# Two transformer blocks on one core: the FFN up-projection meets both halves of its activations in one matmul, the compression runs on unsplit fp32, the keys are padded with zeros

## The chip, the core and the metric

The kernel runs on one core of a Trainium2 chip. A core has a matrix engine (TensorE, PE in the profile; its weight loads stand apart as PEld), a vector engine (VectorE, DVE), a scalar engine (ScalarE, ACT), GpSimd (POOL) and an engine that here only issues DMAs (SyncE, SP). They run side by side and wait for one another through semaphores. The metric is the device time of one execution in microseconds, median of three runs.

## The reference, cut to what matters

256 tokens of width 1024 go through two layers of a first block and two of a second. Everything is fp32. What the change touches:

```python
def compress(t, pe, w1, b1, w2, b2):          # keys and values, per kv group
    ...                                       # 15 blocks of 32 tokens, stride 16
    flat = blocks.transpose(0, 1, 3, 2, 4).reshape(B, nc, G, CMP_LEN * D)   # 2048 wide
    h = jax.nn.gelu(flat @ w1 + b1)           # 2048 -> 256
    return h @ w2 + b2

s_s = einsum('bqgrd,bgqkd->bgrqk', qb, k_g) * scale    # selected keys; 8 heads, 2 key groups of 64
s_w = einsum('bqgrd,bkgd->bgrqk', qb, kwb) * scale     # window keys

def conv_ffn(x, w_up, conv_w, conv_b, w_down):         # first block, D_FF = 2816
    h = x @ w_up                                       # 1024 -> 2 * 2816
    hc = conv_b
    for k in range(CONV_WIDTH):                        # 3 taps along the tokens
        hc = hc + hp[:, k:k + S] * conv_w[k]
    g, up = jnp.split(hc, 2, axis=-1)
    return (jax.nn.silu(g) * up) @ w_down

gu = h @ w_ffn_gu                                      # second block, the same widths, no taps
ffn = (jax.nn.silu(gu[..., :D_FF_2]) * gu[..., D_FF_2:]) @ w_ffn_down
```

## The kernel before

Large products are made in a shortened fp32 (`F32R`). Each fp32 operand is split into a high half and a low half, and a product is the sum of three: high by high, high by low, low by high. `split` makes the halves of a weight tile `raw` of 128x1024 (`wh` by a cast, `wl` by a subtraction), `put_split` those of an activation; these stand in tiles `x` of class `X4`, high and low in a tile each. Small products (attention scores, masks, the second product of the compression) take fp32 as it is, and the profile shows each such matmul as two PE instructions.

`ffn` goes over 22 feature tiles of 128 (`ft`), two to a step. For gate and up (`gu`) it loads 128 columns of `w_up`, splits them, and `up_mm` makes 8 x 3 matmuls of 256 columns (the 256 tokens move, the weight stands still) into one half of a PSUM bank of class `upp`. One DVE instruction takes both halves out of the bank and multiplies them by the rows' norm factor `R`. In the first block come the three taps (`conv`), then silu, the product, the split into `ah` and `al`, and `down_mm`: 12 matmuls of 512 columns per `ft` into four banks, `pa` for the first 128 tokens (`t` = 0) and `pb` for the second. The last four `ft` are held back, and all their `t` = 0 matmuls are asked for before those of `t` = 1, so that the norm of the first tokens can begin early; two of these four have their weights in `x` tiles (`spare`). In the second block the first four `ft` are made another way (`linear`), so 36 of 44 products go through `up_mm` there.

`first_mix` is the attention part of the first block. `compress_g` runs twice a layer: it gathers 30 columns per 128 of the 2048 inputs, splits them, splits four tiles of weights, and makes 16 x 2 matmuls (60 and 30 stationary columns, 256 moving) into one bank; `pair_sum` adds the two halves afterwards. `qk_g` transposes the keys into `kT`, whose rows 0 to 63 are group 0 and rows 64 to 127 group 1, and `attend_g` multiplies 64 rows of `qT` by 64 rows of `kT`.

The order is not the program's. A recorder collects all operations, and `schedule` places them with costs of its own: each engine takes the ready operation of least priority number, which is its place in the program plus an entry of the table `SHIFT`; `HOLD` delays one, and `ALT` names operations that go to another engine (a cast from ACT to DVE, a product from DVE to POOL). Tiles come from classes with a fixed number of slots. Every operation is emitted from one line, so all rows of the profile say L522, and one goes by tile names.

Of the kernel before, what the change touches and what calls it, by code (L numbers as in the profile page):

```python
# [516 lines left out]
def emit(nc, order):  # L517
    for op in order:
# [9 lines left out]
        (0, 0): 11, (0, 2): -701  # L528
    },
# [5 lines left out]
    },  # L535
# [5 lines left out]
    },  # L541
    "f1m": {
        (1, 0): -520, (1, 1): -3630, (1, 2): -723, (2, 0): -251, (2, 1): 188, (2, 2): -699
    },
# [11 lines left out]
    },  # L556
# [5 lines left out]
    },  # L562
    "f2m": {
        (1, 0): -676, (1, 1): -278, (1, 2): -631, (2, 1): -3, (2, 2): -666
    },
# [23 lines left out]
    },  # L589
# [47 lines left out]
    },  # L637
    "s": {
        (0, 0): 76, (0, 2): 156
    },  # L640
    "s2": {
        (0, 0): 185
# [57 lines left out]
        386, (13, 0): 1023, (13, 2): 251, (15, 0): 2398, (15, 1): 1400, (18, 2): 643  # L700
    },
}
ALT = {
    "f1": {
        79, 137, 148, 149, 216, 217
    },
# [1305 lines left out]
```

## Time and profile before

| | |
|---|---|
| median of three runs | 1586.02 us (1585.66 to 1587.5) |
| span of the profiled execution | 1583.9 us |
| of the span, PE busy | 99% |
| DVE, ACT, POOL busy | 68%, 48%, 31% |
| granted PE clock | 1.00 in every stretch but the last (0.97) |
| read from HBM | 267.94 MB |

The runs' median lies 2.1 us above the span, and that is taken to stay. The stages follow one another: mixing of layer 1 to about 153 us, its FFN to 342, its gate, then the same for layer 2 to about 700, then twice mixing (260 us) and FFN of the second block. A busy time on PE counts matmuls that overlap, so the mean of one matmul (283 ns for 256 columns) is not what it costs; that is the distance from its start to the next one's start.

### The profile page before, as it was taken

The numbers are of one execution on the slowest core, as the hardware profiler recorded it, in microseconds if no ns is written. First come the engines' busy times: TensorE is split into PE (matmuls) and PEld (weight loads), VectorE is DVE, ScalarE is ACT, GpSimd is POOL, SyncE is SP. The second block draws the span as 40 slices with busy tenths as digits, with TensorE's granted clock in tenths as the row PEclk, the third lists the DMA queues.
The fourth block names the chain that finished last, engine by engine and source line by source line (L and its number), as shares of the span: only waits on it lengthen the run. The fifth ranks groups of instructions, "written<-read, shape, count | busy, mean of one in ns | idle before, by whom it ended". The sixth has DMA issues, their size and how long they took to land.

```text
span 1583.9 us, 24617 instructions
## 1 busy us (share of the span) xinstructions
PE 1562.3 (99%) x9421; PEld 1358.9 (86%) x9421; DVE 1083.7 (68%) x1582; ACT 761.7 (48%) x1333; POOL 492.3 (31%) x428
## 2 busy tenths in 40 slices
PE   7999999999999999999999999999999999999998
PEld 6778999988778999988888888999988888889997
DVE  6777877888777877886645647566566455675664
ACT  4566555554666545556453444323354534343242
POOL 2433111122433111115233552323443326424233
PEclk9999999999999999999999999999999999999999
DMA  8643765745644656736534556566555344555571
GB/s 271 221 147 103 216 186 176 217 129 172 202 128 129 211 180 189 211 121 194 180 109 132 166 186 193 172 188 188 163 183 186 107 139 160 193 173 174 178 224 38
DMA packets 264091, 270.60 MB, mean 171 GB/s; under 512 B 11698, under 2 KB 196645, under 8 KB 263973
## 3 DMA queue, kind: packets, MB, share of 16 engines
q1 hardware_dynamic: 263972, 269.03, 55.0%
q8 instruction: 74, 1.21, 0.3%
q14 instruction: 45, 0.36, 0.1%
HBM read 267.94 MB, written 1.05 MB: 170 GB/s over the span
## 4 chain that ended last, share of the span: by engine, by line
PE 96%; DVE 2%; ACT 1%; DMA 1%; SPq 0%; issue 0%; POOL 0%; DVEq 0%; POOLq 0%; ACTq 0%
PE pa L522 36%; PE upp L522 35%; PE pb L522 19%; PE trp L522 5%; DMA raw<-in_w_in_dram 1%; DVE wl L522 1%; DVE u L522 1%; SPq L522 0%; ACT L522 0%; ACT u L522 0%; ACT junk L522 0%; DVE x L522 0%; DVE wh L522 0%; ACT x L522 0%; POOL sm L522 0%
## 5 line engine op out<-in xcount | busy, mean ns | idle before, releaser
L522 ACT CAST wh<-raw 128x1024 fp32r<-128x1024 f32 (+3 forms) x382 | 393.0, 1033 | 470.3 <-PE upp L522 234.1
L522 DVE TENSOR_TENSOR wl<-raw,wh 128x1024 fp32r<-128x1024 f32 (+3 forms) x402 | 500.5, 1257 | 119.2 <-ACT wh L522 114.5
L522 PE MATMUL upp<-x,wh 128*128 128x256 f32 x2560 | 479.3, 283 | 0.0
L522 PE MATMUL pa<-wh,x 128*128 128x512 f32 (+1 forms) x1280 | 425.9, 402 | 3.7 <-DVE x L522 2.0
L522 PEld LDWEIGHTS upp<-x,wh 128*128 128x128 f32 x2560 | 406.3, 191 | 6.2 <-ACT wh L522 0.3
L522 PE MATMUL upp<-x,wl 128*128 128x256 f32 x1280 | 361.3, 283 | 1.5 <-DVE wl L522 1.5
L522 POOL TENSOR_TENSOR wl<-raw,wh 128x1024 fp32r<-128x1024 f32 (+2 forms) x94 | 228.7, 2436 | 282.8 <-ACT wh L522 121.7
L522 PEld LDWEIGHTS pa<-wh,x 128*128 128x128 f32 x1280 | 236.7, 189 | 53.2 <-ACT u L522 2.6
L522 PE MATMUL pa<-wl,x 128*128 128x512 f32 (+1 forms) x640 | 251.9, 401 | 0.0
L522 PEld LDWEIGHTS upp<-x,wl 128*128 128x128 f32 x1280 | 244.6, 191 | 3.4 <-DVE wl L522 2.0
L522 POOL TENSOR_TENSOR u<-u,u 128x256 f32<-128x256 f32 (+4 forms) x98 | 109.3, 1117 | 328.0 <-ACT u L522 288.0
L522 DVE CAST wh<-raw 128x1024 fp32r<-128x1024 f32 (+3 forms) x114 | 89.3, 787 | 100.3 <-PE pa L522 38.7
L522 PE MATMUL pb<-wh,x 128*128 128x512 f32 (+2 forms) x496 | 157.4, 384 | 0.0
L522 PEld LDWEIGHTS pa<-wl,x 128*128 128x128 f32 x640 | 120.8, 189 | 21.4 <-DVE u L522 0.8
L522 DVE TENSOR_TENSOR u<-upp,u 128x512 f32<-128x512 f32 x80 | 55.2, 690 | 72.4 <-PE upp L522 71.6
L522 PEld LDWEIGHTS pb<-wh,x 128*128 128x128 f32 x496 | 90.4, 188 | 15.8 <-ACT wh L522 0.6
L522 PE MATMUL pb<-wl,x 128*128 128x512 f32 (+2 forms) x248 | 92.2, 381 | 0.0
L522 PE MATMUL trp<-c_ident,u 128*128 128x128 f32 (+4 forms) x415 | 79.5, 274 | 2.6 <-DMA u<-in_pre_mix_g_dram 1.9
L522 POOL TENSOR_TENSOR sm<-sm,c_nhalf 128x1 f32<-128x1 f32 (+1 forms) x60 | 47.9, 799 | 106.3 <-DVE sm L522 104.3
L522 DVE SCALAR_TENSOR_TENSOR u<-u,c_cols_conv_w,u 128x254 f32<-128x254 f32 (+1 forms) x176 | 73.5, 478 | 0.0
L522 ACT ACTIVATE u<-u 128x256 f32<-128x256 f32 (+1 forms) x100 | 44.5, 445 | 55.5 <-DVE u L522 49.6
L522 POOL TENSOR_TENSOR al<-u,ah 128x256 fp32r<-128x256 f32 x22 | 22.6, 1027 | 148.0 <-ACT ah L522 78.0
(209 smaller groups left out, 2092.3 us busy)
## 6 DMA issues: line engine op xcount, KB each, us to landing
raw<-in_w_in_dram SPq DMA_DIRECT2D x112, 512.0 KB, 4.0
raw<-in_w_up_dram SPq DMA_DIRECT2D x88, 512.0 KB, 4.2
raw<-in_w_ffn_gu_dram SPq DMA_DIRECT2D x88, 512.0 KB, 4.8
raw<-in_w_down_dram SPq DMA_DIRECT2D x44, 512.0 KB, 4.4
raw<-in_w_ffn_down_dram SPq DMA_DIRECT2D x44, 512.0 KB, 4.1
raw<-in_w_o_dram SPq DMA_DIRECT2D x32, 512.0 KB, 4.0
raw<-in_cmp_w_dram SPq DMA_DIRECT2D x16, 512.0 KB, 4.9
raw<-in_w_ple_gate_dram SPq DMA_DIRECT2D x16, 512.0 KB, 3.9
```

The lines of the kernel that those rows point to most:

```text
L522: f(*args, **kw)
```

## The change

- `up_mm`: high and low activations now lie side by side in one tile of class `X8` (four of 2048 in place of nine `X4` of 1024). The high weight meets both in one matmul of 512 columns, the low weight the high half in one of 256. Gate goes to a bank of `upp`, up to one of `trp`; a copy (ACT) and an addition (DVE) join the two halves of each bank, and the multiplication by `R` then reads SBUF.
- `compress_g`: no split. The 30 columns are padded to 32, and 16 fp32 matmuls of 32 stationary columns write four groups of 32 PSUM partitions; `pair_sum` adds the four and now has 128 rows.
- `kT` becomes two tiles, one for each key group, with zeros in the other group's 64 rows; the scores use all 128 rows.
- new tables `SHIFT`, `HOLD`, `ALT`.

```diff
 SHIFT = {
     "c1": {
-        (0, 0): 11, (0, 2): -701
+        (0, 0): 333, (0, 2): -3277
...
-    c["pair_sum"] = np.concatenate([np.eye(30, dtype=f), np.eye(30, dtype=f)], axis=0)
+    c["pair_sum"] = np.concatenate([np.eye(32, 30, dtype=f)] * 4, axis=0)
...
-    X4 = cls("x4", 9, 1024, F32R, reserve=2)
+    X8 = cls("x8", 4, 2048, F32R, reserve=1)
...
     def xtile():
-        xh = X4.tile([128, 4, 256])
-        xl = X4.tile([128, 4, 256])
-        return xh, xl
+        both = X8.tile([128, 4, 2, 256])
+        return both[:, :, 0], both[:, :, 1], both
...
-                nc.tensor.matmul(ps, hv[:, k], xh, start=(k == 0), stop=False)
-                nc.tensor.matmul(ps, hv[:, k], xl, start=False, stop=False)
-                nc.tensor.matmul(ps, lv[:, k], xh, start=False, stop=(k == 7))
+                xx = xs[k // 4][2][:, k % 4]
+                nc.tensor.matmul(ps, hv[:, k], xx.rearrange("p a n -> p (a n)"), start=(k == 0), stop=(k == 7),
+                                 skip_group_check=True)
+                nc.tensor.matmul(ps[:, 0:256], lv[:, k], xx[:, 0], start=False, stop=(k == 7), skip_group_check=True)
...
-                        up_mm(ps[:, gu], hv, lv)
+                        up_mm(ps, hv, lv)
+                        nc.scalar.copy(z[:, gu], ps[:, 256:512])
+                        nc.vector.tensor_tensor(z[:, gu], ps[:, 0:256], z[:, gu], op=ALU.add)
                     if ft == nq:
                         R = spread(rs)
-                    z = unit("z").rearrange("p (a n) -> p a n", a=2)
-                    nc.vector.tensor_tensor(z, ps, bcast(R.unsqueeze(1), [128, 2, 256]), op=ALU.mult)
+                    nc.vector.tensor_tensor(z, z, bcast(R.unsqueeze(1), [128, 2, 256]), op=ALU.mult)
...
-                nc.vector.tensor_copy(kT[:, :, tok(t)], ps[:, 0:2])
+                for g in range(2):
+                    gp, go = slice(g * 64, (g + 1) * 64), slice((1 - g) * 64, (2 - g) * 64)
+                    nc.gpsimd.memset(kT[g][go, :, tok(t)], 0.0)
+                    nc.vector.tensor_copy(kT[g][gp, :, tok(t)], ps[gp, 0:2])
...
-                    hv, lv = split(load(w1[:, m0:m0 + 4]))
-                    for mm in range(4):
-                        m = 8 * mq + 4 * mh + mm
...
-                        nc.tensor.matmul(ps1[:60, :256], xs_[:, m].rearrange("p a n -> p (a n)"), hv[:, mm],
-                                         start=(m == 0), stop=(m == 15))
...
+                raw = load(w1[:, 4 * mq:4 * mq + 4])
+                for r in range(4):
+                    nc.tensor.matmul(ps1[32 * r:32 * r + 32, :256], X[:, 4 * mq + r], raw[:, r], start=(mq == 0),
+                                     stop=(mq == 3))
...
-                    nc.tensor.matmul(S[:, e], qT[t][gp, j0 + e], kT[gp, :, 0:(t + 1) * 128], start=True, stop=False)
+                    nc.tensor.matmul(S[:, e], qT[t][:, j0 + e], kT[g][:, :, 0:(t + 1) * 128], start=True, stop=False)
```

Three places show how the rows move on PE. A row says what is written, then what moves and what stands, and the moving columns. First the up-projection in the FFN of layer 1, before: three matmuls of 256 columns to each of eight pieces of `x`.

```order
L522 MATMUL upp_227<-x_80,wh_65 128x256
L522 MATMUL upp_227<-x_78,wh_65 128x256
L522 MATMUL upp_227<-x_80,wl_70 128x256
L522 MATMUL upp_228<-x_77,wh_68 128x256
L522 MATMUL upp_228<-x_81,wh_68 128x256
L522 MATMUL upp_228<-x_77,wl_74 128x256
```

The three of a piece read two `x` tiles, high and low. The same place of layer 2 in the changed kernel:

```order
L522 MATMUL trp_225<-x_77,wh_68 128x512
L522 MATMUL trp_225<-x_77,wl_73 128x256
L522 MATMUL upp_223<-x_75,wh_65 128x512
L522 MATMUL upp_223<-x_75,wl_70 128x256
...
L522 MATMUL pa_218<-wh_67,ah_107 128x512
L522 MATMUL pa_218<-wl_72,ah_107 128x512
```

Two matmuls remain of three, with the same 768 moving columns, and up-products now take banks of `trp`. Next the compression of layer 1 among the projections, before:

```order
L522 MATMUL pb_226<-wh_66,x_78 128x512
L522 MATMUL trp_230<-wh_67,x_79 60x256
L522 MATMUL trp_230<-wl_72,x_79 30x256 x2
L522 MATMUL trp_230<-wh_67,x_79 60x256
L522 MATMUL trp_230<-wl_72,x_79 30x256
```

Matmuls of 60 and 30 stationary columns alternate in one bank. In the changed kernel:

```order
L522 MATMUL trp_224<-raw_58,u_81 32x256
L522 MATMUL upp_222<-wh_68,x_75 128x280
L522 MATMUL upp_222<-wl_73,x_75 128x280
L522 MATMUL upp_222<-wh_68,x_75 128x280 x2
L522 MATMUL trp_224<-raw_58,u_81 32x256
L522 MATMUL trp_224<-raw_60,u_81 32x256 x4
L522 MATMUL upp_222<-wl_73,x_75 128x280
```

Of the 16 matmuls of this call five stand alone, and the others in runs of five and six; the two calls for the values have one run of nine, one of two and five alone. Last the end of the FFN of layer 1, where the last `ft` (here `wh_69`, `al_117`) meets the first tokens in `pa`, before:

```order
L522 MATMUL pa_223<-wl_71,ah_112 128x512
L522 MATMUL pa_223<-wh_69,al_117 128x512
L522 MATMUL pb_225<-x_75,ah_115 128x512
L522 MATMUL pb_226<-x_75,ah_115 128x512
...
L522 MATMUL pb_225<-wl_71,ah_112 128x512
L522 MATMUL trp_229<-c_ident_190,c_h_191 128x128 x4
```

After `pa` is complete 13 matmuls into `pb` stand ahead of the next norm's transposes (`trp`) and three behind their beginning, 16 in all. In the changed kernel:

```order
L522 MATMUL pa_218<-wl_74,ah_108 128x512
L522 MATMUL pa_218<-wh_69,al_113 128x512
L522 MATMUL pb_220<-wh_69,ah_108 128x512
L522 MATMUL pb_221<-wh_69,ah_108 128x512
L522 MATMUL pb_220<-wl_74,ah_108 128x512
L522 MATMUL pb_221<-wl_74,ah_108 128x512
L522 MATMUL pb_220<-wh_69,al_113 128x512
L522 MATMUL pb_221<-wh_69,al_113 128x512
L522 MATMUL trp_225<-c_ident_185,c_h_186 128x128 x4
```

Six are left: ten of the 16 moved ahead of the last `ft`'s share of `pa`. The end of layer 2's FFN reads the same.

## Rows read from the trace of the kernel before

**Rows 1.** The page: span, busy time of each engine, shares of the chain that ended last.

```profile
span 1583.9 us, 24617 instructions
PE 1562.3 (99%) x9421; PEld 1358.9 (86%) x9421; DVE 1083.7 (68%) x1582; ACT 761.7 (48%) x1333; POOL 492.3 (31%) x428
PE 96%; DVE 2%; ACT 1%; DMA 1%; SPq 0%; issue 0%; POOL 0%; DVEq 0%; POOLq 0%; ACTq 0%
```

**Rows 2.** Stretches: us, busy by engine, granted clock, DMA share, GB/s; FFN of layer 1.

```profile
193.00:313.00 120.00, 120.00 (x846) 112.64 (x845) 94.86 (x138) 61.68 (x93) 15.18 (x13) 1.00 0.64 193
```

**Rows 3.** The chain in order of time: start us, us, engine and tile, matmuls.

```profile
738.35 10.00 PE pa L522 x44
...
1120.55 17.27 PE upp L522 x144
```

**Rows 4.** PE groups by form: rows*columns standing, moving form, count, busy us, mean ns, idle.

```profile
L522 PE MATMUL upp<-x,wh 128*128 128x256 f32 x2560 | 479.3, 283 | 0.0
L522 PE MATMUL upp<-x,wl 128*128 128x256 f32 x1280 | 361.3, 283 | 1.5 <-DVE wl L522 1.5
L522 PE MATMUL upp<-u,u 64*128 64x512 f32 x32 | 17.9, 640 | 0.0
L522 PE MATMUL upp<-u,u 64*128 64x256 f32 x32 | 11.1, 428 | 0.0
```

**Rows 5.** PE in order of time: start us, us, what; scores, fp32 products, `pair_sum`.

```profile
61.27 0.70 PE L522 MATMUL upp<-u,u 64*128 64x256 f32 x2
61.90 0.28 PE L522 MATMUL upp<-c_causal_b,c_ident_b 128*128 128x256 bf16 x1
...
80.21 1.12 PE L522 MATMUL upp<-u,u 64*128 64x512 f32 x2
81.26 1.10 PE L522 MATMUL pb<-u,u 128*128 128x64 f32 x8
...
86.12 0.61 PE L522 MATMUL pa<-wh,x 128*128 128x512 f32 x2
86.67 0.40 PE L522 MATMUL trp<-c_pair_sum,u 60*128 60x30 f32 x2
87.00 0.43 PE L522 MATMUL pb<-u,u 128*128 128x64 f32 x2
...
110.92 1.02 PE L522 MATMUL pa<-u,u 128*128 128x512 f32 x2
111.78 0.27 PE L522 MATMUL trp<-c_ident,u 128*128 128x128 f32 x1
...
830.43 0.59 PE L522 MATMUL upp<-u,c_gla_a 128*128 128x256 f32 x2
830.86 0.38 PE L522 MATMUL trp<-c_ident,u 128*128 128x128 f32 x2
```

**Rows 6.** PE in order of time, compression of layer 1.

```profile
35.69 0.40 PE L522 MATMUL pb<-wh,x 128*128 128x512 f32 x1
35.92 0.28 PE L522 MATMUL trp<-wh,x 128*60 128x256 f32 x1
36.04 0.40 PE L522 MATMUL trp<-wl,x 128*30 128x256 f32 x2
36.28 0.28 PE L522 MATMUL trp<-wh,x 128*60 128x256 f32 x1
```

**Rows 7.** DVE and ACT groups by form: count, busy us, mean ns, idle and its releaser.

```profile
L522 DVE TENSOR_TENSOR u<-upp,u 128x512 f32<-128x512 f32 x80 | 55.2, 690 | 72.4 <-PE upp L522 71.6
...
L522 DVE TENSOR_TENSOR u<-u,upp 128x256 f32<-128x256 f32 x8 | 3.3, 418 | 1.6 <-ACT u L522 1.6
...
L522 ACT COPY u<-trp 128x256 f32<-128x256 f32 x4 | 1.5, 369 | 1.6 <-PE trp L522 1.6
```

**Rows 8.** PE in order of time, end of the FFN of layer 1.

```profile
337.07 0.39 PE L522 MATMUL pa<-wh,al 128*128 128x512 f32 x1
...
342.73 0.47 PE L522 MATMUL pa<-wh,x 128*128 128x512 f32 x1 [0.75 <-DVE x L522]
```

More of the change, by code (lines that the diff above doesn't have):

```diff
@@ L527 @@
     "c1": {
-        (0, 0): 11, (0, 2): -701
+        (0, 0): 333, (0, 2): -3277
     },
     "f1": {
[4 rows of a table removed]
[4 rows of a table added]
     },
     "f1e": {
[4 rows of a table removed]
[4 rows of a table added]
     },
     "f1m": {
-        (1, 0): -520, (1, 1): -3630, (1, 2): -723, (2, 0): -251, (2, 1): 188, (2, 2): -699
+        (1, 0): -2776, (1, 1): -12192, (1, 2): -723, (2, 0): -132, (2, 1): 65, (2, 2): -699
     },
     "f2": {
[10 rows of a table removed]
[10 rows of a table added]
     },
     "f2e": {
[4 rows of a table removed]
[4 rows of a table added]
     },
     "f2m": {
-        (1, 0): -676, (1, 1): -278, (1, 2): -631, (2, 1): -3, (2, 2): -666
+        (1, 0): 3800, (1, 1): -303, (1, 2): 1273, (2, 0): 56, (2, 1): 5016, (2, 2): 505
     },
     "m1": {
[22 rows of a table removed]
[20 rows of a table added]
     },
     "m2": {
[39 rows of a table removed]
[37 rows of a table added]
     },
     "p1": {
[5 rows of a table removed]
[5 rows of a table added]
     },
     "s": {
-        (0, 0): 76, (0, 2): 156
+        (0, 0): 122, (0, 2): 230
     },
     "s2": {
-        (0, 0): 185
+        (0, 0): 3778, (0, 2): 419
     },
@@ L646 @@
     "c1": {
-        (0, 0): 974, (0, 2): 1486
+        (0, 0): 240, (0, 2): 1072
     },
     "f1": {
-        (3, 1): 62, (5, 0): 106, (5, 2): 7, (6, 2): 1094, (9, 2): 18, (12, 2): 519, (14, 1): 1238
+        (2, 2): 281, (3, 0): 135, (4, 2): 40, (5, 1): 366, (5, 2): 7, (6, 0): 3301, (6, 2): 155, (9, 2): 84,
+        (14, 1): 14
     },
     "f1e": {
-        (1, 0): 569, (1, 1): 203, (2, 1): 693, (3, 0): 782, (6, 0): 548, (10, 2): 7, (11, 2): 115, (12, 2): 256,
-        (14, 2): 270
+        (1, 0): 153, (2, 0): 1771, (2, 1): 13, (3, 1): 1007, (5, 1): 568, (6, 2): 49, (9, 2): 178, (11, 2): 250
     },
     "f1m": {
-        (1, 0): 1474, (1, 1): 252, (2, 1): 275
+        (1, 0): 95, (1, 1): 302, (2, 1): 664
     },
     "f2": {
[4 rows of a table removed]
[4 rows of a table added]
     },
     "f2e": {
-        (1, 1): 953, (2, 1): 1454, (3, 1): 191, (4, 1): 75, (5, 1): 294
+        (1, 1): 1210, (2, 1): 1691, (6, 0): 6, (8, 2): 293, (9, 2): 53, (10, 2): 174, (11, 2): 566, (14, 2): 49
     },
     "f2m": {
-        (1, 0): 3995, (1, 1): 715, (2, 1): 268
+        (1, 0): 1, (2, 0): 1479, (2, 1): 1079
     },
     "m1": {
[8 rows of a table removed]
[7 rows of a table added]
     },
     "m2": {
[15 rows of a table removed]
[14 rows of a table added]
     },
     "p1": {
-        (3, 2): 15, (6, 2): 4, (8, 0): 580, (8, 1): 2246, (10, 0): 1337, (10, 1): 3584, (11, 2): 70, (12, 1):
-        386, (13, 0): 1023, (13, 2): 251, (15, 0): 2398, (15, 1): 1400, (18, 2): 643
+        (3, 2): 452, (7, 1): 2054, (8, 1): 1387, (9, 0): 2083, (9, 1): 981, (10, 1): 2524, (12, 1): 1580, (13,
+        0): 2016, (13, 1): 200, (13, 2): 266, (15, 1): 2721, (18, 2): 502, (20, 2): 167
+    },
+    "s2": {
+        (0, 0): 1073
     },
@@ L703 @@
 ALT = {
+    "c1": {
+        10, 13
+    },
     "f1": {
-        79, 137, 148, 149, 216, 217
+        8, 11, 12, 61, 79, 82, 121, 127, 138, 164, 182, 194, 196
     },
     "f1e": {
-        28, 62, 224, 302, 303, 306, 336, 371, 372, 439, 504
+        1, 50, 51, 119, 120, 155, 176, 188, 244, 256, 311, 335, 367, 432
     },
     "f1m": {
-        62, 81, 142
+        110, 118
     },
     "f2": {
-        17, 31, 32, 39, 53, 145, 167, 168, 170, 226, 228, 230, 238, 279, 307, 308, 311, 349, 350, 405, 424, 482,
-        483, 520, 575, 576, 580, 621, 622, 649, 654, 674, 747, 765, 792, 793, 821, 822, 824, 896, 940, 968, 969,
-        972, 973
[3 rows of a table added]
     },
     "f2e": {
-        56, 57, 76, 103, 132, 206, 278, 280, 286, 312, 340, 342, 374, 402, 403, 407
+        19, 23, 44, 46, 106, 108, 143, 147, 168, 169, 170, 208, 209, 226, 231, 232, 237, 255, 259, 278, 280,
+        281, 309, 326, 331, 334
     },
     "f2m": {
-        1, 28, 57, 58, 76, 130, 131, 134
+        1, 22, 44, 45, 48, 49, 63, 64, 81, 102, 107, 110
     },
     "m1": {
[4 rows of a table removed]
[4 rows of a table added]
     },
     "m2": {
[6 rows of a table removed]
[7 rows of a table added]
     },
     "p1": {
-        5, 16, 32, 35, 37
+        12, 16, 31, 32, 37, 69
     },
     "s": {
-        5, 6, 9, 11
+        5, 11, 12
     },
     "s2": {
-        7, 18, 19, 21, 27, 34, 35, 36, 43
+        18, 19, 21, 32, 33, 34, 35
     },
@@ L966, in split @@
         a, n = v.shape[1], v.shape[2]
-        wh = (X4 if spare else WH).tile([128, 1024])
-        wl = (X4 if spare else WL).tile([128, 1024])
+        if spare:
+            both = X8.tile([128, 2, 1024])
+            wh, wl = both[:, 0], both[:, 1]
+        else:
+            wh, wl = WH.tile([128, 1024]), WL.tile([128, 1024])
         hv = wh[:, :a * n].rearrange("p (a n) -> p a n", a=a)
@@ L991, in mms @@
                 k = k0 + a
-                xh, xl = xs[k // 4]
+                xh, xl = xs[k // 4][:2]
                 lh, ll = xh[:, k % 4, tok(t)], xl[:, k % 4, tok(t)]
@@ L1040, in feat @@
             nc.tensor.transpose(ps[:, a], s, ident)
-        xh, xl = xt
+        xh, xl = xt[:2]
         if gains is None:
@@ L1211, in ffn @@
                 rec.group += 1
-                ps = bank(upp, "upps").rearrange("p (a n) -> p a n", a=2)
                 act = unit("act")[:, :256]
@@ L1215, in ffn @@
                 if ft >= nq:
+                    z = unit("z").rearrange("p (a n) -> p a n", a=2)
                     for gu in range(2):
                         c0 = gu * DFF + ft * 128
+                        ps = bank(trp if gu else upp, "upps")
                         hv, lv = split(load(wu[:, :, c0:c0 + 128]))
-                        up_mm(ps[:, gu], hv, lv)
+                        up_mm(ps, hv, lv)
+                        nc.scalar.copy(z[:, gu], ps[:, 256:512])
+                        nc.vector.tensor_tensor(z[:, gu], ps[:, 0:256], z[:, gu], op=ALU.add)
                     if ft == nq:
                         R = spread(rs)
-                    z = unit("z").rearrange("p (a n) -> p a n", a=2)
-                    nc.vector.tensor_tensor(z, ps, bcast(R.unsqueeze(1), [128, 2, 256]), op=ALU.mult)
+                    nc.vector.tensor_tensor(z, z, bcast(R.unsqueeze(1), [128, 2, 256]), op=ALU.mult)
                 else:
+                    ps = bank(upp, "upps").rearrange("p (a n) -> p a n", a=2)
                     for gu in range(2):
@@ L1295, in first_mix @@
         linear(xs, 8, w, 512, 1024, put_kv, pool=pa)
-        qT, kT = [], unit("kT").rearrange("p (b n) -> p b n", b=2)
+        qT, kT = [], [unit("kT").rearrange("p (b n) -> p b n", b=2) for g in range(2)]
         gates = []
@@ L1333, in compress_g @@
                     nc.tensor.transpose(ps[:, g, tok(t)], zC[t][:, a * 128:(a + 1) * 128], ident)
-            X = unit("X")
-            Xv = X[:, :480].rearrange("p (m g n) -> p m g n", m=16, g=2)
+            X = unit("X").rearrange("p (m c) -> p m c", m=16)
+            nc.gpsimd.memset(X[:, :, 30:32], 0.0)
+            Xv = X[:, :, 0:30].rearrange("p m (g n) -> p m g n", g=2)
             pe = col("cmp_pe", i, kv * 16, 16)
@@ L1345, in compress_g @@
             yield
-            xs_ = X4.tile([128, 16, 2, 30])
-            Xm = X[:, :480].rearrange("p (m n) -> p m n", m=16)
-            nc.scalar.copy(xs_[:, :, 0], Xm)
-            nc.vector.tensor_tensor(xs_[:, :, 1], Xm, xs_[:, :, 0].bitcast(F32), op=ALU.subtract)
             yield
@@ L1352, in compress_g @@
             ps1 = bank(trp, "cps")
-            for mq in range(2):
-                for mh in range(2):
-                    m0 = 8 * mq + 4 * mh
-                    hv, lv = split(load(w1[:, m0:m0 + 4]))
-                    for mm in range(4):
-                        m = 8 * mq + 4 * mh + mm
-                        if m > 0:
-                            nc.tensor.matmul(ps1[:30, :256], xs_[:, m, 0], lv[:, mm], start=False, stop=False)
-                        nc.tensor.matmul(ps1[:60, :256], xs_[:, m].rearrange("p a n -> p (a n)"), hv[:, mm],
-                                         start=(m == 0), stop=(m == 15))
-                        if m == 0:
-                            nc.tensor.matmul(ps1[:30, :256], xs_[:, m, 0], lv[:, mm], start=False, stop=False)
-                    yield
-            h1 = unit("h1")[:60, :256]
-            nc.scalar.copy(h1, ps1[:60, :256])
+            for mq in range(4):
+                raw = load(w1[:, 4 * mq:4 * mq + 4])
+                for r in range(4):
+                    nc.tensor.matmul(ps1[32 * r:32 * r + 32, :256], X[:, 4 * mq + r], raw[:, r], start=(mq == 0),
+                                     stop=(mq == 3))
+                yield
+            h1 = unit("h1")[:, :256]
+            nc.scalar.copy(h1, ps1[:, :256])
             psh = bank(trp, "hps")
@@ L1419, in attend_g @@
                 g, j0 = divmod(h0, 4)
-                gp = slice(g * 64, (g + 1) * 64)
                 S = bank(upp, "S").rearrange("p (e b n) -> p e b n", e=nh, b=2)
                 for e in range(nh):
-                    nc.tensor.matmul(S[:, e], qT[t][gp, j0 + e], kT[gp, :, 0:(t + 1) * 128], start=True, stop=False)
+                    nc.tensor.matmul(S[:, e], qT[t][:, j0 + e], kT[g][:, :, 0:(t + 1) * 128], start=True, stop=False)
                     mask_add(S[:, e, :, t * 128:(t + 1) * 128], 2)
```

2 lines of the change are left out of this document (removed), and 248 rows, old and new, of tables (ALT, HOLD, SHIFT).

## The prediction

> **What bounds the kernel now.** I read the page first: PE is busy 99% of a span of 1583.9 us, and the chain that ended last is 96% PE [rows 1]. So what PE issues is the time, and the other engines count only where they make it wait. Next come the stretches: in the FFN of layer 1 PE is busy for all of 120 us at full clock, DVE for 94.86 and ACT for 61.68 of them [rows 2]. The groups by form show PE idle ahead of the up-products for 0.0 and 1.5 us over 3840 matmuls [rows 4], and DVE waits for PE there, 71.6 us over 80 times [rows 7]. The FFN is bound by PE's issue, then. Last I took the cost of a matmul from the chain, as time over count: 10.00 us over 44 for 512 columns, 0.2273 us each, and 17.27 over 144 for 256 columns, 0.1199 each [rows 3]. Twice the columns cost 1.90 times as much, so each matmul carries some 0.0125 us that its columns don't explain. A change that makes fewer matmuls of the same columns gains that much for each.
>
> **Up-projection.** A piece of `x` costs 3 x 0.1199 = 0.3598 us before, and 0.2273 + 0.1199 = 0.3472 after: 0.0126 less. There are 3840 / 3 = 1280 pieces [rows 4]. Sum: -16.1 us. The ends: if the wide matmul cost two narrow ones, 0; below -16.1 the rows give no reason.
>
> What it adds lies on other engines. Each `ft` gets two additions of 256 columns out of PSUM on DVE, 0.418 us each, and two copies on ACT, 0.369 each; the multiplication by R stays (0.690 now) and reads SBUF [rows 7]. A conv `ft` takes 48 x 0.1199 + 12 x 0.2273 = 8.48 us on PE, and DVE's share of 94.86 / 120 makes 6.70 us of it. After, PE needs 16 x 0.3472 + 2.73 = 8.28 us, and DVE 6.70 + 0.84 = 7.54, or 91%. ACT goes from 4.36 to 5.10. Both still end inside PE's time, so I cost the additions at nothing. If that cover went, DVE's excess over 8.28 us would be paid 44 times; that is the rival on the other side below. The banks are no new wait: gate takes one of two `upp` banks and up one of two `trp` banks, so a bank comes back after two `ft`, 16.6 us.
>
> **Keys.** Two matmul rows of 64 stationary rows and 512 columns take 81.26 - 80.21 = 1.05 us, 0.525 each; with 128 rows two take 111.78 - 110.92 = 0.86, 0.430 each. At 256 columns it is (61.90 - 61.27) / 2 = 0.315 against (830.86 - 830.43) / 2 = 0.215 [rows 5]. There are 32 of each [rows 4]: 32 x 0.095 + 32 x 0.100 = 6.2 us. The matmul ahead of a low one is late too: the two `pa` ahead of `pair_sum` (60 rows) take 86.67 - 86.12 = 0.55 us where two cost 0.455, so 0.09 is lost at the change of height [rows 5]. The scores come in 32 such places, 2.9 us. Together -9.1 us, with 0 as the other end of the 2.9. The zeros and the second key copy are eight small instructions each on POOL and DVE off this path; at nothing, since PE has other projections in its order there.
>
> `pair_sum` becomes 128 rows high: two of its rows take 87.00 - 86.67 = 0.33 us [rows 5], and no matmul of 256 columns or fewer in the compression costs over 0.12 [rows 6]; with the 0.09 ahead, 0.33 + 0.09 - 0.24 = 0.18, eight times: -1.4 us.
>
> **Compression.** Before, 4 calls x 32 matmuls at (36.28 - 36.04) / 2 = 0.12 [rows 6] are 15.4 us. After, 4 x 16 fp32 matmuls of two PE rows at 0.215 [rows 5], if they follow one another, are 27.5 us: +12.1. No row shows two column groups at work at once. If four could run together wherever they stand together, the order leaves nine turns of 0.43 per call, 15.5 us: 0. In between: the two rows of one matmul use the same columns and must follow each other, but the second may run beside the first row of the next; a run of n then costs n + 1 rows, and 23 rows a call make 4 x 23 x 0.215 = 19.8 us. I take this one, +4.4 us, since it lies between and needs only that rows start in order, as all of them do in the trace; both ends go into the range. The 16 splits that fall away take work from ACT and DVE, which are not the bound; at nothing.
>
> On the change of width the rows say: 35.92 - 35.69 = 0.23 us for the full-width matmul ahead of the first of 60 columns, no more than its 0.2273, and 0.12 where 60 and 30 alternate [rows 6]. The Trainium skill (TensorEngine Tiling, Tiling Modes) says that a change of tiling mode, as against a change of tile, drains TensorE. For heights the trace agrees, with 0.09 us [rows 5]; for widths it does not. By that rule the 28 runs of the changed compression would pay 28 x 2 x 0.09 = 5 us more.
>
> **End of the conv FFN.** The chain from the PSUM bank to `al` of the last `ft` grows by a copy, an addition and their hand-overs, and the order answers by moving ten `pb` matmuls ahead of the last share of `pa`. In the trace `pa` is complete at 337.07 + 0.39 = 337.46, and the gate's first matmul starts at 342.73, after 0.75 us of idle [rows 8]. Those 5.27 us are the norm of the first tokens, which doesn't shorten, and the ten matmuls no longer fill it: 10 x 0.2273 = 2.3 us more idle, at both conv FFNs: +4.5 us (0 if the norm is ready sooner, 9 if the gate slips twice that far). The two FFNs of the second block keep their fill there.
>
> **Sum.** -16.1 - 9.1 - 1.4 + 4.4 + 4.5 = -17.7 us. The span goes from 1583.9 to 1566.2, and with the 2.1 us that lie around it the median to 1568. The new tables move waits elsewhere too. The loads of the second block stand in the same sequence, and so do nearly all of the first; I add 0 with 5 us either way.
>
> **Rivals.**
> - Column groups follow one another: +12.1 in place of +4.4, 1576 us. For it: no row of before shows overlap. Against: separate columns and separate PSUM partitions leave nothing that the trace shows them to share. Chance 0.2.
> - Column groups run four at a time, or the conv ends cost nothing: 1564, both 1559. For the first: as above. For the second: a scheduler that moved ten matmuls forward may have had the norm's time to spare. Chance 0.27.
>
>   The Trainium skill (TensorEngine Tiling, Tiling Modes) states that different tiles can load weights and multiply in parallel; no run here shows it so far. By it the compression costs 0 and the time is 1564.
> - The additions make DVE the bound of the conv FFN. It decides from 8.28 us of DVE work per `ft`. At the row means it is 7.54; if its new neighbours (copies on ACT, products on POOL) made every DVE instruction 20% longer, 9.05 us, the excess of 0.77 x 44 = 34 us would turn -17.7 into +16: 1602. For it: from 79% to 91% is a large step. Against: a row's busy time contains the overlap with the next, so 91% overstates. Chance 0.04.
> - The wide up-matmul costs two narrow ones (0.2398): -1.6 in all, 1584. Against: 512 columns cost 0.2273 wherever they stand in the trace. Chance 0.03.
>
> **How the numbers follow.** The forecast as summed has 0.43 and by itself reaches from 1562 to 1574 (the 5 us of the tables and part of the conv ends). The remaining 0.03 are unknown waits of a new order. The range from 1556 to 1580 holds the forecast, nearly all of the two rivals on the compression, and leaves out DVE as the bound and the empty change. About 3 us (0.2%) is what a measurement of this kernel can tell from no change. Faster: 0.43 + 0.2 + 0.27 and part of the unknown, 0.92; same 0.03; slower 0.05.
>
> **What would show it.** PE rows: 640 + 640 up-matmuls of 512 columns, and a chain in which 16 of 512 and 256 mixed take 2.78 us. The stretch of a conv `ft` shrinks from 8.48 to 8.28. Scores at 0.43 and 0.215 with no late matmul ahead. The 128 rows of the compression: their starts 0.215 apart, or nearly together. At the gate's start an idle of about 3 us. I am wrong if PE shows idle ahead of the up-products (the banks), or if DVE's waits for PE there are gone.

## The result: slower by 0.76%, and the profile after

The changed kernel takes 1599.09 us (1595.89 to 1599.76, 4 runs), the kernel before 1586.76 in the same session: ratio 1.0076, interval 1.0062 to 1.0089. The forecast was 1568. First the page of the changed kernel, beside [rows 1]:

```profile
span 1597.5 us, 22249 instructions
...
PE 1562.1 (98%) x8141; PEld 1287.5 (81%) x8141; DVE 1181.8 (74%) x1821; ACT 739.3 (46%) x1371; POOL 543.0 (34%) x447
...
PE 92%; DVE 2%; ACT 2%; POOL 1%; DMA 1%; issue 1%; SPq 0%; DVEq 0%; POOLq 0%; ACTq 0%
```

PE has 1280 instructions fewer and is no less busy; its share of the chain falls from 96% to 92%. So the matmuls shrank and waits came in. To see where, I took from each trace the time from the start of a matmul to the start of the next and added it up by kind:

| us from start to start | before | after | change | forecast |
|---|---|---|---|---|
| up-products | 462.8 | 453.3 | -9.5 | -16.1 |
| scores | 26.9 | 21.5 | -5.4 | -9.1 |
| `pair_sum` | 2.6 | 1.3 | -1.3 | -1.4 |
| compression | 15.6 | 19.1 | +3.5 | +4.4 |
| down-products | 246.4 | 255.4 | +9.0 | |
| other products with weights | 664.4 | 674.8 | +10.4 | |
| products with the identity (transposes, masks) | 65.7 | 69.9 | +4.2 | |
| ahead of the first matmul, and the rest | 92.6 | 95.1 | +2.5 | |

The first four give 12.7 us. The last four, whose instructions did not change, take 26.1 more, where the forecast had 4.5. To see in which stages the waits lie, I took each time from start to start less the median of its form, and added up what exceeds 0.15 us (late starts from here on; slow matmuls at 1.2 GHz are in them): 8.4 us more than before at the starts of the two conv FFNs, 9.7 at their ends, 6.0 in the two mixings of the first block, and nothing in the middle of the conv FFNs.

The middle of the conv FFN has no waits, as forecast, but gains less. The stretch of [rows 2], with DVE at 98.84 of 120 us; then two links of the chain (start us, us, engine and tile, matmuls) two `ft` apart, in the changed kernel and before:

```profile
193.00:313.00 120.00, 120.00 (x634) 102.62 (x633) 98.84 (x161) 77.25 (x128) 21.19 (x15) 1.00 0.67 198
```

```profile
198.06 2.83 PE upp L522 x16
...
214.85 2.83 PE upp L522 x16
```

```profile
193.55 6.83 PE upp L522 x57
...
210.61 6.83 PE upp L522 x57
```

Eight wide and eight narrow matmuls take 2.83 us, where 2.78 was forecast. Two `ft` take 16.79 us, before 17.06; twice the forecast 8.28 is 16.56. PE's groups by form, beside [rows 4]: no idle ahead of the up-products, and the scores have 128 rows.

```profile
L522 PE MATMUL upp<-x,wh 128*128 128x512 f32 x640 | 231.8, 397 | 0.1
...
L522 PE MATMUL upp<-x,wl 128*128 128x256 f32 x640 | 179.5, 281 | 0.5 <-DVE wl L522 0.5
...
L522 PE MATMUL upp<-u,u 128*128 128x512 f32 x32 | 17.7, 641 | 0.1
...
L522 PE MATMUL upp<-u,u 128*128 128x256 f32 x32 | 9.2, 379 | 0.0
```

At the edges of the FFN PE waits. The end of layer 1's FFN on PE in order of time (in brackets the idle ahead and what ended it), beside [rows 8]:

```profile
345.37 0.61 PE L522 MATMUL pb<-wh,al 128*128 128x512 f32 x2
347.67 1.29 PE L522 MATMUL trp<-c_ident,c_h 128*128 128x128 f32 x8 [1.68 <-DVE c_h L522]
350.14 0.80 PE L522 MATMUL pa<-wh,x 128*128 128x512 f32 x1 [1.18 <-ACT x L522]
```

Two waits in place of one, 2.86 us against 0.75. During the second the clock falls. Three stretches of the same kernel; the column behind POOL's is the granted clock:

```profile
346.00:349.50 3.50, 1.26 (x8) 0.84 (x8) 3.11 (x6) 3.44 (x10) 1.77 (x6) 1.00 0.34 128
349.50:356.30 6.80, 6.16 (x15) 4.74 (x16) 6.35 (x11) 0.96 (x3) 2.23 (x3) 0.50 0.45 125
356.30:366.00 9.70, 9.70 (x48) 8.08 (x47) 5.12 (x9) 4.75 (x8) 2.16 (x3) 1.00 0.17 52
```

PE works 1.26 of 3.50 us, and for the next 6.8 us it has 1.2 GHz. This happens again at 711 us (the other gate), at 540 and at 472 us, some 20 us in all. In the profiled execution of the kernel before the clock stood at 2.4 GHz in all these places and fell only after PE's last matmul. The start of the conv FFN, on PE and on POOL:

```profile
177.66 0.40 PE L522 MATMUL pa<-wh,ah 128*128 128x512 f32 x1
179.82 0.50 PE L522 MATMUL pa<-wh,al 128*128 128x512 f32 x1 [1.75 <-POOL al L522]
```

```profile
177.13 2.63 POOL L522 TENSOR_TENSOR al<-u,ah 128x256 fp32r<-128x256 f32 x1 [11.85 <-ACT ah L522]
```

PE stands 1.75 us for a product that an entry of `ALT` gave to POOL. At 540 us the same wait is followed by the clock's fall, here it is not.

### The profile page after: what moved, and what is told of

Same layout as the page of the kernel before. It is cut to its first block, busy times and chain, and to the rows that moved or that the text cites. A ratio compares the mean times of both kernels' runs of the same rounds, so it can differ in the third digit from the quotient of the medians.

```text
span 1597.5 us, 22249 instructions
## 1 busy us (share of the span) xinstructions
PE 1562.1 (98%) x8141; PEld 1287.5 (81%) x8141; DVE 1181.8 (74%) x1821; ACT 739.3 (46%) x1371; POOL 543.0 (34%) x447
## 4 chain that ended last, share of the span: by engine, by line
PE 92%; DVE 2%; ACT 2%; POOL 1%; DMA 1%; issue 1%; SPq 0%; DVEq 0%; POOLq 0%; ACTq 0%
PE pa L522 35%; PE upp L522 19%; PE pb L522 19%; PE trp L522 18%; DMA raw<-in_w_in_dram 1%; DVE u L522 1%; ACT wh L522 1%; POOL sm L522 1%; POOL al L522 1%; ACT junk L522 1%; ACT u L522 0%; SPq L522 0%; POOL u L522 0%; DMA u<-in_p_dram 0%; DVE x L522 0%
## 5 line engine op out<-in xcount | busy, mean ns | idle before, releaser
L522 ACT CAST wh<-raw 128x1024 fp32r<-128x1024 f32 (+1 forms) x348 | 358.4, 1033 | 477.0 <-PE pa L522 130.6
L522 DVE TENSOR_TENSOR wl<-raw,wh 128x1024 fp32r<-128x1024 f32 (+2 forms) x378 | 472.9, 1260 | 87.0 <-ACT wh L522 85.1
L522 POOL TENSOR_TENSOR wl<-raw,wh 128x1024 fp32r<-128x1024 f32 (+1 forms) x102 | 253.1, 2487 | 256.2 <-ACT wh L522 127.3
L522 PE MATMUL upp<-x,wh 128*128 128x512 f32 x640 | 231.8, 397 | 0.1
L522 PE MATMUL trp<-x,wh 128*128 128x512 f32 x640 | 228.8, 395 | 0.0
L522 PE MATMUL upp<-x,wl 128*128 128x256 f32 x640 | 179.5, 281 | 0.5 <-DVE wl L522 0.5
L522 PE MATMUL trp<-x,wl 128*128 128x256 f32 x640 | 178.4, 280 | 0.0
L522 DVE CAST wh<-raw 128x1024 fp32r<-128x1024 f32 (+2 forms) x132 | 107.0, 813 | 65.9 <-PE pb L522 20.5
L522 PEld LDWEIGHTS upp<-x,wh 128*128 128x128 f32 x640 | 119.6, 188 | 26.9 <-DVE x L522 1.0
L522 PEld LDWEIGHTS pa<-wl,x 128*128 128x128 f32 x640 | 120.6, 190 | 21.6 <-DVE wl L522 1.0
L522 PEld LDWEIGHTS upp<-x,wl 128*128 128x128 f32 x640 | 120.6, 188 | 6.5 <-DVE wl L522 1.2
L522 PEld LDWEIGHTS trp<-x,wl 128*128 128x128 f32 x640 | 120.7, 189 | 2.9
```

The lines of the kernel that those rows point to most:

```text
L522: f(*args, **kw)
```

## The experiments

"In the order of before" means: each operation's priority is the planned start of its counterpart in the kernel before, so no new table decides. "Searched" means: many tables were tried, and the one with the least idle of PE by the kernel's own planner was taken. Each ratio is against before in the same session.

| run | us | ratio, interval |
|---|---|---|
| p_keys | 1579.2 | 0.9958, 0.9944 to 0.9972 |
| p_compress | 1588.4 | 1.0024, 1.0011 to 1.0037 |
| p_up | 1606.1 | 1.0137, 1.0121 to 1.0152 |
| u_short | 1576.5 | 0.9934, 0.9913 to 0.9956 |
| u_load | 1582.9 | 0.9973, 0.9961 to 0.9986 |
| u_ends | 1584.6 | 0.9994, 0.9978 to 1.0010 |
| after_tab | 1590.2 | 1.0019, 1.0006 to 1.0032 |
| after_fill | 1593.7 | 1.0042, 1.0028 to 1.0056 |
| after_al | 1596.5 | 1.0064, 1.0049 to 1.0079 |
| after_al1 | 1591.0 | 1.0031, 1.0019 to 1.0043 |
| uk_all | 1588.5 | 1.0005, 0.9992 to 1.0019 |
| uk_mid | 1569.2 | 0.9876, 0.9852 to 0.9901 |
| uk_mid4 | 1578.0 | 0.9930, 0.9906 to 0.9955 |
| before_own | 1581.4 | 0.9973, 0.9963 to 0.9983 |
| all_mid | 1581.9 | 0.9980, 0.9970 to 0.9989 |
| all_mid2 | 1592.9 | 1.0043, 1.0026 to 1.0060 |

**Which part loses: p_keys, p_compress, p_up.** One part of the diff each, in the order of before.

```diff
+nc.tensor.matmul(S[:, e], qT[t][:, j0 + e], kT[g][:, :, 0:(t + 1) * 128], start=True, stop=False)   # p_keys
+nc.tensor.matmul(ps1[32 * r:32 * r + 32, :256], X[:, 4 * mq + r], raw[:, r], ...)                   # p_compress
+nc.scalar.copy(z[:, gu], ps[:, 256:512])                                                            # p_up
```

> The kernel before with the zero-padded keys alone; every operation is asked for in the order that the kernel before had, so no new table is in it. Theory O (the parts gain what their matmuls save, and the new order of the changed kernel lost it): the scores' two PE rows go from 0.525 to 0.43 and from 0.315 to 0.215 us, no matmul ahead of a score loses 0.09; 5 to 9 us faster than before, ratio 0.994 to 0.997. Theory P (a part itself costs more than it saves): same or slower.

> The kernel before with the compression on unsplit fp32 in four column groups and pair_sum of 128 rows alone, in the order of the kernel before. Theory O: the compression's PE time goes from 15.6 to about 19 us, pair_sum gives 1.3 back; 2 to 3 us slower than before (ratio 1.001 to 1.002), or no change that can be told. Theory P: 8 us slower or more (groups one after the other, 12 us).

> The kernel before with the side-by-side up-projection alone (compression and keys as before), in the order of the kernel before as far as the longer chain behind the up-products allows. Theory O: the up-products' own starts lie 0.233 and 0.118 us apart, 10 us less than before over 1280 pieces; what makes it slower than that is PE idle at the ends of the FFNs, where the added copy and addition come late, and clock lost behind it; between 1580 and 1605 us, the sum of PE's waits over 0.1 us 15 to 30 us above before. Theory P: the wide matmul with its bank in two halves costs what two narrow ones cost, and the time is slower with waits as before.

The keys gain 6.5 us, the compression loses 2.8 and the up-projection 20.5. The first two times lie in the ranges of their Theory O; p_up's lies 1 us above its range. So the keys gain what their matmuls save, and most of the loss sits in the up-projection, without any new table. The end of layer 1's FFN in p_up, on PE and on ACT:

```profile
338.95 0.61 PE L522 MATMUL pb<-wh,al 128*128 128x512 f32 x2
341.90 0.47 PE L522 MATMUL pa<-wh,ah 128*128 128x512 f32 x1 [2.33 <-DVE ah L522]
...
345.85 0.63 PE L522 MATMUL pb<-wh,al 128*128 128x512 f32 x2
349.63 1.09 PE L522 MATMUL trp<-c_ident,c_h 128*128 128x128 f32 x4 [3.15 <-DVE c_h L522]
```

```profile
339.61 1.04 ACT L522 CAST wh<-raw 128x1024 fp32r<-128x1024 f32 x1 [2.59 <-PE pb L522]
340.56 0.41 ACT L522 ACTIVATE u<-u 128x256 f32<-128x256 f32 x1
```

The last `ft`'s silu (340.56) stands on ACT behind a cast that waits for PE, and PE in turn waits for `ah`, which comes from the silu; then PE waits 3.15 us for the norm.

In p_compress the time came as expected, but by luck: the compression itself took less PE time than before, 11.9 us where about 19 were expected and 15.6 stood before. The loss is late starts: 8.3 and 3.4 us more of them than before in the two mixings of the first block. PE there, and then in the changed kernel:

```profile
36.86 0.40 PE L522 MATMUL pb<-wh,x 128*128 128x512 f32 x1
37.18 0.64 PE L522 MATMUL trp<-raw,u 128*32 128x256 f32 x8
37.75 0.50 PE L522 MATMUL pb<-wh,x 128*128 128x512 f32 x1
```

```profile
34.05 0.62 PE L522 MATMUL trp<-raw,u 128*32 128x256 f32 x2
34.60 0.73 PE L522 MATMUL pb<-wh,x 128*128 128x512 f32 x2
```

Four fp32 matmuls in four column groups (eight rows) take 0.57 us, and one alone (two rows) takes 0.55. The unmerged rows of the trace say why: in a run of four the first rows start 7 ns apart, so the groups run together. The Trainium skill (TensorEngine Tiling (Array Packing), Tiling Modes) says that different tiles can run in parallel, and the trace now agrees. The wide matmul ahead takes 0.32 us in place of 0.23, so the change into column groups costs 0.09. The Trainium skill (TensorEngine Tiling (Array Packing), Tiling Modes) says that a change of mode drains TensorE, and the 0.09 us agree with it. The prediction had found it not to hold for widths, but from outputs of 60 and 30 columns that use no column groups. In the changed kernel's order 20 of the 64 compression matmuls stand alone, at 0.55 us each; they are 11.0 of its 19.1 us.

**The chain or the load: u_short, u_load.**

```diff
-nc.scalar.copy(z[:, gu], ps[:, 256:512])
-nc.vector.tensor_tensor(z[:, gu], ps[:, 0:256], z[:, gu], op=ALU.add)
-nc.vector.tensor_tensor(z, z, R, op=ALU.mult)
+nc.vector.tensor_tensor(z[:, gu], pss[gu][:, 0:256], R, op=ALU.mult)                          # u_short, u_load
+nc.scalar.copy(side[:, gu], pss[gu][:, 256:512])                                              # u_load
+nc.vector.tensor_tensor(side[:, gu], pss[gu][:, 0:256], side[:, gu], op=ALU.add)              # u_load
```

> p_up with the chain behind the up-products as short as before: R multiplies the first 256 columns straight out of each bank, and the copy and the addition are gone. The product of the high weight and the low activation half is made and left out of the result. Theory O (the waits come from the two added links of the chain): the stalls of p_up in the FFNs (5.2, 11.3, 4.6, 8.0, 7.4 and 7.5 us in its stretches) fall back to those of before (0.8, 1.9, 0.8, 2.2, 2.8, 2.9), the clock stays up, and the time is 8 to 11 us below before, 1575 to 1578. Theory Q (the waits come from the two banks that each ft now takes, or from the wide matmul itself): at most a few us better than p_up's 1606.

> u_short (R multiplies straight out of the banks) with the copy and the addition of each bank put back as side work: ACT and DVE make them into a tile that nothing reads, asked for later than the chain. The low activation half is left out of the result as in u_short. It has the engine load of p_up without the two links in the chain. Theory L (the length of the chain is the price): 1577 to 1584, within 8 us of u_short's 1576.5. Theory D (DVE and ACT have no room for the 0.84 and 0.74 us per ft, or the banks come back late): 1595 or more, near p_up's 1606.

Without the two links the up-projection gains 9.3 us; with them it loses 20.5. They cost 29.7 us (1606.1 - 1576.5), of which 6.5 come back as load alone (1582.9) and 23 are the length of the chain; both figures hold what the clock's falls cost (while PE worked, 17 us at 1.2 GHz in p_up, 10 in u_load and none in u_short). The 6.5 don't lie in the middle either: the late starts are 5.0 and 4.9 us at u_load's two conv ends, and 1.2 at each before. The gate's start in u_short is what it was before; in u_load PE waits there for DVE:

```profile
338.64 0.40 PE L522 MATMUL pb<-wh,al 128*128 128x512 f32 x1
339.77 0.47 PE L522 MATMUL pa<-wh,x 128*128 128x512 f32 x1 [0.74 <-DVE x L522]
```

```profile
343.83 0.50 PE L522 MATMUL pa<-wh,x 128*128 128x512 f32 x1 [2.19 <-DVE x L522]
```

**The order of the changed kernel: after_tab, after_fill, after_al, after_al1.**

```diff
 "f1": { ...
-        8, 11, 12, 61, 79, 82, 121, 127, 138, 164, 182, 194, 196
+        8, 11, 12, 61, 79, 82, 121, 127, 138, 164, 182, 196                                   # after_al
+eng = "vector" if op.key[:2] == ("f1", 138) else op.eng                                       # after_al1, in emit
+FILL = {("p1", 0): 13, ("p1", 41): 9}                                                         # after_fill, in emit
+nc.tensor.transpose(o, ident, ident)                                                          # after_fill, 13 and 9 times
```

> The changed kernel with other tables SHIFT, HOLD, ALT and nothing else: searched with the kernel's own planner for less planned idle of PE. Theory O: most of PE's added waits were a matter of order; 10 to 20 us below the changed kernel, 1579 to 1589. Theory S (the longer chain forces these waits in any order): within 4 us of the changed kernel's 1599.

> The changed kernel with PE kept at work in its two idle times at the start of each gate: 13 transposes of the identity ahead of the first transpose of the tokens, 9 ahead of the gate's first matmul (their results are overwritten). The waits themselves stay. Theory C (the clock fell because PE stood idle there): the two stretches of 6.83 us at 1.2 GHz are gone and the time falls by 5 to 8 us, to 1591 to 1594. Rival: the clock falls there for another reason, and the time stays within 2 us of 1599.

> The changed kernel with one entry fewer in ALT: the low half of the second ft's activation (al) of each conv FFN is made on DVE and no longer on POOL, where it took 2.63 us and PE stood 1.75 us for it. If that placement made the wait: the waits at 178 and 538 us go, with the clock's drop at 540 us, 3 to 6 us faster than the changed kernel (1593 to 1596). If the chain is late anyway: no change, 1597 to 1600.

> The changed kernel in its own order, all instructions at their places, but the low half of the first ft's activation in each conv FFN (the al for which PE stood 1.75 us at 178 and 540 us) is made by DVE at its place in the order and not by POOL. after_al had moved the one of the second ft instead. If the placement made the wait: it falls below 0.6 us at both places, 2 to 5 us faster than the changed kernel (1594 to 1597). If the chain is late anyway: DVE reaches it no sooner than POOL did, no change.

Other tables alone gave 9 of the 12 us back (after_tab, a little short of what was expected). The fill gave 5.4 us by the ratios (1.0076 to 1.0042). PE at the gate and the clock in that kernel:

```profile
346.48 1.58 PE L529 MATMUL trp<-c_ident 128*128 128x128 f32 x13
348.23 1.38 PE L533 MATMUL trp<-c_ident,c_h 128*128 128x128 f32 x8 [0.17 <-DVE c_h L533]
349.44 1.15 PE L529 MATMUL pa<-c_ident 128*128 128x128 f32 x9
350.79 0.50 PE L533 MATMUL pa<-wh,x 128*128 128x512 f32 x1 [0.20 <-ACT x L533]
```

```profile
342.50:349.00 6.50, 6.24 (x37) 5.04 (x35) 5.27 (x10) 4.79 (x11) 1.99 (x6) 1.00 0.41 136
349.00:356.00 7.00, 6.64 (x33) 4.99 (x34) 6.56 (x12) 1.71 (x5) 2.23 (x3) 1.00 0.35 112
```

The gate starts no sooner, and the clock stays at 2.4 GHz, so at these gates the clock's fall came with PE's idle time. The 5.4 us are not the gates' alone: in this execution the clock stayed up at the other two places too, though nothing was filled there and the second layer's wait for `al` remained (1.76 us). And idle time does not always bring the fall: in after_al1 the first gate has the same two waits and keeps its clock.

```profile
346.85 1.29 PE L523 MATMUL trp<-c_ident,c_h 128*128 128x128 f32 x8 [1.68 <-DVE c_h L523]
349.32 0.50 PE L523 MATMUL pa<-wh,x 128*128 128x512 f32 x1 [1.18 <-ACT x L523]
```

```profile
349.30:356.00 6.70, 6.52 (x29) 4.65 (x30) 6.17 (x11) 0.88 (x3) 2.23 (x3) 1.00 0.52 153
```

after_al is a miss: it moved the second `ft`'s `al`, and PE waits for the first's. after_al1 moved the right one, with all else in its place, and gained 7 us by the ratios, more than the 2 to 5 expected and more than the two waits of 1.75. In the profiled execution the clock fell less often too (3.4 us at 1.2 GHz while PE worked, in place of 20). How much of the gain that is stays open, since executions of after_al1 with a granted clock of 0.995 took 1590.7 to 1591.9 us and those with 0.998 took 1589.5 to 1591.1. PE and DVE there:

```profile
178.68 0.39 PE L523 MATMUL pa<-wh,ah 128*128 128x512 f32 x1
178.91 0.39 PE L523 MATMUL pa<-wh,al 128*128 128x512 f32 x1
```

```profile
178.10 0.43 DVE L523 TENSOR_TENSOR al<-u,ah 128x256 fp32r<-128x256 f32 x1 [0.26 <-ACT ah L523]
```

**Can the chain be kept off the edges: u_ends, uk_all, uk_mid, uk_mid4.** A feature tile is made wide, or as before by three narrow matmuls, by its place in the FFN. uk_mid and uk_mid4 have the keys as well, uk_all has keys and wide `ft` throughout; these three have a searched order.

```diff
+WIDE = ((2, 16), (2, 16))          # uk_mid; u_ends and uk_mid4: ((4, 16), (6, 16))
+wide = n0 <= fts.index(ft) < n1
```

> p_up with the first four and the last six ft of each conv FFN, the first two and last six up-projected ft of the other FFNs done by three narrow matmuls into one bank as before (40 of 80 up-projected ft stay side by side). Theory O: the waits at the ends of the FFNs go, half the saving stays: 4 to 6 us below before, 1580 to 1582. Theory Q: between before and p_up in proportion to the wide ft, about 1596.

> Side-by-side up-projection in all ft and the zero-padded keys, compression as before, with an order of its own, searched from the order of before for less planned idle of PE. Theory S (the longer chain forces its waits in any order): keys give 6.5 us on p_up's 1606, so 1597 or more. Theory O2 (order can hide most of them): 1575 to 1585; the stalls at the conv FFNs' ends fall from 11 and 8 us to under 5.

> As uk_all, but the first two and the last six places of each FFN go by three narrow matmuls with the short chain (50 of the 80 up-projected ft stay side by side), with an order of its own found in the same way. Theory O2 and L both: keys -6.5, 50/80 of the 9.7 us that the up-products save, waits as before: 1570 to 1575, faster than both kernels. If the chain costs in the middle of the FFN too: 1576 to 1582.

> As uk_mid with 40 of the 80 ft side by side (first four and last six places of the conv FFNs, first and last six of the others narrow). 1.2 us less saved than uk_mid by the matmuls; if the edges of the FFNs still cost in uk_mid, faster than it, else 1 to 2 us slower: 1571 to 1576.

uk_mid, a little better than expected, is faster than both kernels, by 1.2% and 1.9%:

```profile
span 1567.0 us, 23170 instructions
...
PE 1549.6 (99%) x8621; PEld 1317.5 (84%) x8621; DVE 1184.6 (76%) x1744; ACT 768.7 (49%) x1391; POOL 477.8 (30%) x420
```

u_ends cannot be told from before (1.2 us less, and its interval reaches across 1) where 4 to 6 us were expected: its gates start as before, but late starts of 0.9 us in each conv FFN and 2.3 in each FFN of the second block (0 and 0.9 before) stayed in the middle. So in the order of before the chain is not wholly free there. uk_all, with a searched order, still loses 10.2 us at each of the two conv ends (late starts; 10.5 and 8.3 in p_up, 1.2 at each before), so order did not hide the chain at these ends. It does hide part of the whole: p_up's loss falls from 20.5 to 9 us (1588.5 + 6.5 for the keys - 1585.7), between the two theories. uk_mid4 was to lie within 2 us of uk_mid and is 9 us slower; its search put waits of 1.5 to 2.3 us into the mixings of the second block, whose matmuls the change leaves as they were. A searched order can cost as much as the matmuls give.

**What the search is worth: before_own, all_mid, all_mid2.** Only the order of before, searched; and uk_mid with the compression.

```diff
+if rhs.tile.cls.name == "raw": d = 150.0                                  # all_mid, all_mid2: planner's cost
-return n * (2.2 if two else 0.95) + 120.0, None
+return (n * 1.55 + 800.0 if two else n * 0.95 + 120.0), None              # all_mid2: POOL's price
```

> The kernel before with nothing changed but the order, searched in the same way and for as long as that of uk_mid (the planner's planned end falls by 2.3 us, for uk_mid it had fallen by 14). If uk_mid's 16.5 us come from its matmuls (keys 6.5, 50 of 80 up-projected ft side by side 6), this stays within 4 us of before, 1582 to 1588. If they come from the search, it falls to 1575 or less.

> uk_mid with the changed kernel's compression too, so all three parts, with the planner told that a compression matmul takes 150 ns beside its neighbours, and an order searched in the same way. In p_compress the compression and pair_sum took 5.0 us less of PE than before and the order gave 7.5 back. With an order made for it: 2 to 5 us below uk_mid, 1564 to 1567. If its waits come back in any order (raw tiles held by the matmuls, loads late): 1569 or more.

> all_mid with the planner told what a product of two tiles takes on POOL in the traces (256 columns 1.0 to 1.5 us, 512 columns 1.4 to 1.6 us; it had reckoned with 0.68 and 1.25), and the order searched again. If all_mid lost to uk_mid because of products put on POOL that PE then waited for (2.0 us at the start of each conv FFN, 0.4 us in each further step): those waits go, 1564 to 1572, level with uk_mid or below. If the compression's part costs it in any order: 1576 or more.

Search alone gains 4.3 us, at the edge of what was expected. If it is worth the same in uk_mid, which no run shows, 12 of uk_mid's 16.5 us are its matmuls, and the sum agrees: 6.5 from the keys and 5.8 (50/80 of 9.3) make 12.3. all_mid missed the 1564 to 1567 of its first theory; PE at the start of its FFN:

```profile
155.52 0.28 PE L524 MATMUL upp<-x,wl 128*128 128x256 f32 x1
157.67 0.49 PE L524 MATMUL trp<-u,c_ones 128*128 128x128 f32 x2 [1.86 <-POOL u L524]
```

all_mid2 has none of these waits for POOL and is slower still, with waits in the mixings (2.31 us for a `wh` of ACT at 31 us, 1.9 for `c_h` at 954). Whether the compression's 5 us of PE time can be had in a better order stays open.

## Why the prediction was wrong, step by step

- **The step that failed** is "both still end inside PE's time, so I cost the additions at nothing". It asked whether DVE and ACT had room per `ft`, which they have (DVE 98.84 of 120 us), and not when each result is wanted. In the middle of the FFN a late `ah` costs little, since PE has other up-products. At its start and end there are none, and every hand-over is waited for: 18 us more of late starts there than before, none in the middle of the conv FFN. The chain alone costs 23 us and the load 6.5 in the order of before (p_up against u_load and u_short); the changed kernel itself was not run with the short chain, so how its own loss divides between chain and tables is not shown. The rival on the other side had DVE's load as its mechanism, paid in every `ft`; that did not come. The prediction's first sign of being wrong, PE idle ahead of the up-products, looks at the middle too and stayed silent (0.1 and 0.5 us).
- **End of the conv FFN, +4.5.** The place was right (an idle of 2.86 us at the gate, about 3 forecast), but it was one edge of several, and the clock's falls were not priced: after_fill, which had none of them while PE worked, is 5.4 us faster.
- **New tables, 0 ± 5.** Too narrow. after_tab gives 9 us for tables alone, after_al1 7 us for one product in each conv FFN. The prediction priced no entry of `ALT`, and no step of it asked what a moved product takes on the other engine and who waits for it there.
- **Up-projection, -16.1.** Mechanism right, size off: 9.3 us in u_short. A wide and a narrow matmul into one bank take 0.350 us by their medians (0.233 + 0.117), against 0.347 forecast; of the 1280 x 0.0098 = 12.5 us that this leaves, the up-products of the changed kernel show 9.5. The rival that the wide one costs two narrow ones (0.2398) is refuted.
- **Keys, -9.1.** 6.5 us in p_keys, which is what the rows of the scores give there (26.9 to 20.4 us). The entry loss ahead of them, 2.9 us of the forecast, is gone on many rows (the mask's matmul ahead of a score goes from 0.21 to 0.11 us), but the time shows no gain from it: in p_keys the other products with weights take 2.0 us longer.
- **`pair_sum`, -1.4:** 1.3. Right.
- **Compression, +4.4:** 3.5, the right size by luck. A run of n does not cost n + 1 rows: in the changed kernel a run of five takes 0.98 us where six rows of 0.215 make 1.29, and one matmul alone 0.55 where two rows make 0.43. Groups of four cost what one costs, which is the first half of the rival with the chance of 0.27, and the order decides how many there are.

In all, some 31 us lie between forecast span and measured span: 6.6 on the up-products, 3.7 on the keys, 21.6 on waits and clock, less 0.9 on the compression.

## What to carry to other kernels

In this kernel a link added to a chain behind PE came nearly free only where PE had other work queued: price it at the first and last tiles of the loop, where the queue is empty, and not by the engines' load in the middle. There the old, shorter form can stay, and the cheaper matmul is used between. The order has to be right as well: the same idea gave 1.2, 7.7 and 16.5 us in three orders (u_ends, uk_mid4 and uk_mid, the last two with the keys). When a change brings new order tables, read which instructions change engines and take their time on the new engine from the trace.

## What the runs showed of the hardware

- The same product `al` (128x256) on POOL took 0.737 to 2.635 us in the changed kernel:

```profile
L522 POOL TENSOR_TENSOR al<-u,ah x32: 737/1140/2635, 177.1 to 1576.8; 128x256 fp32r<-128x256 f32 x32
```

  During the 2.63 us at 177.13 DVE ran instructions with two SBUF inputs. The Trainium skill (GPSIMD Engine Reference, Specifications) says that POOL and DVE share their SBUF interfaces and contend there for such instructions. The four that took 1.8 us or more agree, as they ran beside such DVE instructions for 85% of their time or more. Two of 0.738 us do not, as they ran beside one for 86% of theirs, and no run here took DVE's work away.
- A single fp32 matmul of 32 columns takes as long (0.55 us) as four in four column groups (0.57).
- One idle time of 1.75 us on PE was followed by 3.4 us at 1.2 GHz in one layer and by none in the other, with the same instructions. The clock also fell where PE had not waited in the 5.6 us ahead, in the mixing of layer 1 in u_load (the column behind POOL's is the granted clock); in the profiled execution of before it stayed up there.

```profile
100.00:105.60 5.60, 5.60 (x33) 3.48 (x32) 4.29 (x9) 2.71 (x8) 2.25 (x4) 1.00 0.73 211
105.60:109.10 3.50, 3.50 (x9) 1.78 (x9) 1.83 (x4) 1.03 (x3) 0.93 (x3) 0.51 0.41 121
```
